# One written order for the transfers of both queues, and the convolution in forty groups of eight tokens

## The chip, the core and the metric

The kernel runs on one core of one Trainium2 chip. Its time is the device time of one execution in microseconds (us). Engines are named as in the profile: PE (matmuls), DVE (vector), ACT (scalar), POOL, and SP, which only issues transfers here. Transfers are issued from two queues, that of SP and that of ACT.

## What is computed

One step of a hybrid decoder layer for 320 tokens of 1024 features: 256 tokens of one prompt (T columns 0 to 255) and eight samples of eight tokens (columns 256 to 319). The layer is attention over blocks of cached keys and values beside a state-space mixer (SSD), then cross attention to a memory, then a squared-ReLU MLP. The x, B and C rows of the mixer go through a causal depthwise convolution of width 4 before the scan; each sequence starts from its own history of three rows (zeros for the prompt, a cached state for each sample), and the last three raw rows of each sequence are an output:

```python
def causal_conv(xbc, buf, w, bias):
    t = xbc.shape[1]
    full = jnp.concatenate([buf.astype(xbc.dtype), xbc], axis=1)
    y = bias
    for i in range(CONV_W):
        y = y + full[:, i:i + t] * w[i]
    return y, full[:, full.shape[1] - (CONV_W - 1):]
...
x ; x += W_out[concat(MoBA heads, Mamba-2 SSD heads)](rmsnorm(x)) ; x += memory cross-attention(rmsnorm(x), rmsnorm(mem)) ; x += squared-ReLU MLP(rmsnorm(x))
```

## The kernel before

Features lie on the 128 partitions and tokens along the columns. Every gemm multiplies a weight chunk of 128 x 1024 values with eight tiles of 128 x 320. To keep float32 accuracy both sides are split into a rounded part and a remainder, and each product takes three matmuls (`gemm3`, L389 to L391: high by high, high by low, low by high).

A weight chunk of 512 KB is brought by `load` (L331) into one of three buffers `wr`. ACT then makes the rounded part `wh` (L383) and DVE the remainder `wl` (L384). Chunks 5 to 47 are issued from ACT's queue, ahead of the instructions that ACT has behind them, the others from SP's. Cached keys (`ckT`) and values (`cv`) of the sample attention come in 256 KB pieces through SP (L827, tile `kv`).

The program up to the MLP is written as some twenty streams that yield after each portion: V the value projection, Q the query and key gemms, F the query and key factors, S and T the attention of the samples and of the prompt, B the gemms of the x, B and C rows, Z those of the gate, D and R the scan, O and J the output projection, others for memory and cross attention. The string `ORDER` says which stream goes on next (`weave_by`); that sets PE's order. For ACT and DVE two further tables, `ACT_ORDER` and `DVE_ORDER`, give the order of all their instructions. At the end `_issue_order` puts the instructions of one engine in that order. Each engine takes its instructions in that order, and one that waits holds all behind it. ACT's queue of transfers is part of this: a weight issue that has to wait holds the activations behind it.

A transfer signals its landing on one of eight completion semaphores (DMAHW0 to DMAHW7), which are handed out in turn to the transfers of both queues in the order in which the scheduler lists them. A transfer is issued when the one that had the same semaphore before it, eight places ahead in that list, has landed, and when its buffer is free.

For each of its eight tiles of 128 rows, stream B ends in `xbc_done` (L981 on): DVE scales the gemm's result into a row of raw values (L988 for the prompt, L989 for the samples with their eleven columns each), POOL puts the history in and takes the output rows out (L987, L990, L991), ACT starts the sum with the first tap (Identity, L994), DVE adds three taps (L996), ACT makes the tanh (L998), and DVE multiplies (L1003 prompt, L1004 samples).

Other lines that the prediction speaks of: L367 transposes on PE, of the rows s4 that ACT copies (`rows_out`, L505 and L507) or of the sample attention's yn (ACT, L956); L500 sums of squares on PE; L868 the samples' scores on PE, after DVE's block mask m (L872); L893 the samples' probabilities p on ACT; L784 to L790 the prompt's exponentials tq; L881 and L607 small DVE steps of the scores and of the key factors (ts); L1065 PE's first use of the last convolution tiles.

## Time and profile before

| | us |
|---|---|
| median of 3 runs | 520.6 |
| lowest and highest | 519.11, 522.63 |
| profiled execution | 520.65 |
| span of that execution in the trace | 518.9 |
| busy: PE, DVE, ACT, POOL | 501.1, 343.4, 251.5, 48.4 |

The span runs from the first to the last recorded instruction of the program; 1.75 us of the profiled execution lie around it. A row of a group shows its line, engine and operation, what it writes and reads with the shape, how often, then the sum of its time (us) and the mean of one (ns), and behind the last bar the idle time ahead of it and what ended it. A row of the chain shows a start, a length and what ran. The granted clock of PE is full (1.00) throughout.

### The profile page before, as it was taken

Reading aid. Unit: us, or ns where it says so; the run is one execution under the profiler, and the core shown is the slowest. Engines: PE = TensorE matmul, PEld = TensorE weight load, DVE = VectorE, ACT = ScalarE, POOL = GpSimd, SP = SyncE. Lnnn points to the kernel's source line nnn. Section 1 sums busy time; section 2 is a strip of 40 time slices with the busy share of each in tenths; the row PEclk is TensorE's granted clock in tenths of the full one; section 3 lists DMA queues with packets and bytes.
Section 4 is the critical chain, followed back from the end, with each engine's and each line's share of the span. In section 5 each row is a group of like instructions: output and inputs, shape, how many; then the busy total and the mean of one; then the engine's idle time right before and its main releaser. Section 6 shows DMA issues by size and latency. Waiting matters only on the chain.

```text
span 518.9 us, 10547 instructions
## 1 busy us (share of the span) xinstructions
PE 501.1 (97%) x3954; PEld 453.6 (87%) x3954; DVE 343.4 (66%) x713; ACT 251.5 (48%) x512; POOL 48.4 (9%) x98
## 2 busy tenths in 40 slices
PE   8999899997989999999899999999999999999997
PEld 5988677876758799999579899999999999999997
DVE  6867699668668598965748779776766434334431
ACT  7524346947767775735466444343434322332330
POOL 2500000120100000000000122231312000000000
PEclk9999999999999999999999999999999999999999
DMA  8889998999799434796922366564644444544520
GB/s 288 314 304 377 392 351 289 338 329 365 279 377 346 139 123 163 242 332 215 378 93 85 121 248 205 162 222 143 227 140 157 162 147 163 176 149 161 176 95 13
DMA packets 45364, 116.53 MB, mean 225 GB/s; under 512 B 5058, under 2 KB 7234, under 8 KB 45314
## 3 DMA queue, kind: packets, MB, share of 16 engines
q1 hardware_dynamic: 39266, 94.37, 52.8%
q10 hardware_dynamic: 6048, 21.50, 11.5%
q8 instruction: 31, 0.51, 0.4%
q14 instruction: 19, 0.16, 0.1%
HBM read 109.71 MB, written 6.14 MB: 223 GB/s over the span
## 4 chain that ended last, share of the span: by engine, by line
PE 78%; DVE 8%; ACT 6%; DMA 5%; issue 2%; SPq 0%; ACTq 0%; POOL 0%; POOLq 0%
PE mm L389 21%; PE mm L390 20%; PE mm L391 20%; DMA kv<-ckT 3%; PE ms L367 2%; ACT wh L383 2%; DVE wl L384 2%; DMA wr<-w 2%; PE as L921 2%; PE sc L706 1%; PE as L367 1%; PE ms L534 1%; PE sc L868 1%; PE mm L1623 1%; PE sc L1549 1%
## 5 line engine op out<-in xcount | busy, mean ns | idle before, releaser
L383 ACT ACTIVATE wh<-wr 128x1024 fp32r<-128x1024 f32 (+1 forms) x115 | 118.8, 1036 | 175.0 <-PE mm L390 104.9
L384 DVE TENSOR_TENSOR wl<-wr,wh 128x1024 fp32r<-128x1024 f32 (+1 forms) x115 | 144.7, 1261 | 83.5 <-ACT wh L383 81.0
L389 PE MATMUL mm<-big,wh 128*128 128x320 f32 x544 | 171.9, 316 | 2.4 <-DVE t L881 0.7
L390 PE MATMUL mm<-big,wh 128*128 128x320 f32 x544 | 168.2, 309 | 0.0
L391 PE MATMUL mm<-big,wl 128*128 128x320 f32 x544 | 168.2, 309 | 0.0
L389 PEld LDWEIGHTS mm<-big,wh 128*128 128x128 f32 x544 | 102.2, 188 | 9.6 <-issue 5.7
L390 PEld LDWEIGHTS mm<-big,wh 128*128 128x128 f32 x544 | 102.2, 188 | 0.8 <-DVE big L1611 0.3
L391 PEld LDWEIGHTS mm<-big,wl 128*128 128x128 f32 x544 | 102.1, 188 | 0.2 <-DVE wl L384 0.2
L391 PE MATMUL mm<-hh,wl 128*128 128x320 f32 x256 | 78.9, 308 | 0.0
L390 PE MATMUL mm<-hl,wh 128*128 128x320 f32 x256 | 78.9, 308 | 0.0
L389 PE MATMUL mm<-hh,wh 128*128 128x320 f32 x256 | 78.9, 308 | 0.0
L390 PEld LDWEIGHTS mm<-hl,wh 128*128 128x128 f32 x256 | 48.1, 188 | 0.0
L389 PEld LDWEIGHTS mm<-hh,wh 128*128 128x128 f32 x256 | 48.1, 188 | 0.0
L391 PEld LDWEIGHTS mm<-hh,wl 128*128 128x128 f32 x256 | 48.1, 188 | 0.0
L1686 POOL TENSOR_TENSOR t<-t 128x320 f32<-128x320 f32 x32 | 27.8, 869 | 171.3 <-DVE t L1683 162.4
L1683 DVE SCALAR_TENSOR_TENSOR t<-mm,rb 128x320 f32<-128x320 f32 x32 | 15.7, 489 | 15.3 <-PE mm L391 14.8
L996 DVE SCALAR_TENSOR_TENSOR t<-t,cwh,t 128x344 f32<-128x344 f32 x24 | 13.8, 573 | 7.7 <-ACT t L994 7.3
L868 PE MATMUL sc<-kv,qs 128*32 128x256 f32 x256 | 15.9, 381 | 2.3 <-DVE m L872 2.3
L1687 DVE TENSOR_TENSOR hl<-t,hh 128x320 fp32r<-128x320 f32 x32 | 15.4, 481 | 2.5 <-POOL t L1686 2.5
L1684 ACT ACTIVATE hh<-t 128x320 fp32r<-128x320 f32 x32 | 14.6, 458 | 2.5 <-DVE t L1683 2.5
L921 PE MATMUL as<-kv,p 128*32 128x256 f32 x256 | 15.9, 382 | 0.0
L1349 DVE TENSOR_TENSOR x2T<-mm,x2T 128x320 f32<-128x320 f32 x8 | 3.9, 492 | 17.8 <-PE mm L391 17.8
(358 smaller groups left out, 624.0 us busy)
## 6 DMA issues: line engine op xcount, KB each, us to landing
wr<-w SPq DMA_DIRECT2D x69, 512.0 KB, 3.5
wr<-w ACTq DMA_DIRECT2D x41, 512.0 KB, 5.6
kv<-ckT SPq DMA_DIRECT2D x64, 256.0 KB, 5.3
kv<-cv SPq DMA_DIRECT2D x64, 256.0 KB, 5.8
kv<-mk SPq DMA_DIRECT2D x8, 512.0 KB, 6.1
kv<-mv SPq DMA_DIRECT2D x8, 512.0 KB, 7.8
kv<-h SPq DMA_DIRECT2D x4, 512.0 KB, 7.7
big<-h SPq DMA_DIRECT2D x4, 512.0 KB, 5.3
```

Source lines behind the costliest of these rows:

```text
L367: PE.transpose(out, in_, ident[:n, :n])
L383: A.activation(hi[:, c], raw[:, c], AF.Copy)
L384: V.tensor_tensor(lo[:, c], raw[:, c], hi[:, c], op=ALU.subtract)
L389: PE.matmul(out, hi[:, cols], xh, start=start, stop=False)
L390: PE.matmul(out, hi[:, cols], xl, start=False, stop=False)
L391: PE.matmul(out, lo[:, cols], xh, start=False, stop=stop)
L868: PE.matmul(ps[r:r + 32, 256 * n:256 * n + 256], qs[:, s, g, b0 + e, :], kbs[e][:, :, 128 * (2 * g + s):128 * (2 * g + s) + 128], start=s ...
L921: PE.matmul(yv[r:r + 32, 0:256], pT[:, 2 * n + q, r:r + 32], vbs[e][:, q, 256 * g:256 * g + 256], start=n == 0 and q == 0, stop=first and ...
L1683: V.scalar_tensor_tensor(t, ps[:, :T], 0.0, rb3, op0=ALU.max, op1=ALU.mult)
L1684: A.activation(hh[:, m, :], t, AF.Square)
L1686: G.tensor_tensor(f, t, t, op=ALU.mult)
L1687: V.tensor_tensor(hl[:, m, :], f, hh[:, m, :], op=ALU.subtract)
```

## The change

There are three parts.

The new table `DMA_ORDER` lists the transfers of both queues in one order, and `_issue_order` is called for them as well; it takes a condition in place of an engine. So the table decides which earlier transfer each one takes its semaphore from.

`xbc_done` lays the raw values out as 40 groups of 11 columns, each with three columns of history and eight tokens; the 256 prompt tokens are 32 such groups. The history of the prompt's groups 1 to 31 is the end of the group before and is copied by ACT (a new instruction of 128 x 31 x 3). One DVE product fills all groups. The sum starts with the last tap in place of the first, and all steps run over 320 columns where they ran over 344; the last product is one instruction where it was two. POOL has three copies and fills a tile where it had four.

`ORDER`, `ACT_ORDER` and `DVE_ORDER` are new. Lines below the tables stand four further down (L331 is L335 after the change, L383 is L387, L505 is L509, L956 is L960).

```diff
@@ -67,45 +67,49 @@
...
-ORDER = ("VVFVVQQQQQQQQQQQQQQQVFVQFVQFFQQQQFVQQQQQSSQQQFSSQQZQZQSSFSFSSSFFBBBBSZBBSBBFSBBTZSBSSBBBSSTBBTBTBBSS"
...
-ACT_ORDER = ("1 0 2 19 3+1 20 6 5 7 21 8+3 22 12+3 23 16+2 24+2 28 30 33 32 27 37 34 29 43 38 31 50 39 44 36 35 53 59 40+1 "
...
+ORDER = ("FVVVVQQQQQQQQQQQQQVQQFVQFVFQFQQQFVQQQQQSSQQQFSSQQQZQZSSFSFSVSSQFFBBBBSZBSBFBBSBBTZSBSSBBBSSBBTBTTBBS"
...
+ACT_ORDER = ("1 0 2 19 3+1 20 6 5 7 21 8+1 22 10+5 23 18 16+1 24+2 28 30 33 32 27 37 34 29 47 38 31 50 41 48 36 35 57 39+1 "
...
+DMA_ORDER = ("0+15 19+1 16+2 21+2 29+1 27 31+6 28 38+16 64 24 55+1 65 25 66 57+4 75 26 62 67+6 84 74 76+7 63 86+1 85 88+3 "
...
@@ -235,9 +239,9 @@
     return out
 
 
-def _issue_order(tc, nc, eng, runs):
-
-    ins = [i for i in nc.cur_bb.bb.instructions if i.engine == eng and i.is_tile_traced]
+def _issue_order(tc, nc, take, runs):
+
+    ins = [i for i in nc.cur_bb.bb.instructions if i.is_tile_traced and take(i)]
     ins = [ins[i] for i in _runs(runs)]
     info = mybir.DependencyInfo(mybir.DependencyClass.NoSync, mybir.DependencyReason.DATA)
     for a, b in zip(ins, ins[1:]):
@@ -981,27 +985,20 @@
     def xbc_done(m):
         def done(ps):
             cvo = made["cvo"]
-            raw = tm(347)
-            rs3 = raw[:, 259:347].rearrange("p (b t) -> p b t", t=11)
-            G.memset(raw[:, 0:3], 0.0)
-            G.tensor_copy(rs3[:, :, 0:3], scv[:, 24 * m:24 * m + 24].rearrange("p (b t) -> p b t", t=3))
-            V.tensor_tensor(raw[:, 3:259], ps[:, :TP], rb[:, :TP], op=ALU.mult)
-            V.tensor_tensor(rs3[:, :, 3:11], by_seq(ps[:, TP:T]), by_seq(rb[:, TP:]), op=ALU.mult)
-            G.tensor_copy(cvo[:, m, 0:3], raw[:, 256:259])
-            G.tensor_copy(cvo[:, m, 3:27].rearrange("p (b t) -> p b t", t=3), rs3[:, :, 8:11])
-
-            y = tm(344)
-            A.activation(y, raw[:, 0:344], AF.Identity, scale=cwh[:, 4 * m:4 * m + 1], bias=cwh[:, 32 + m:33 + m])
-            for w in range(1, 4):
-                V.scalar_tensor_tensor(y, raw[:, w:w + 344], cwh[:, 4 * m + w:4 * m + w + 1], y, op0=ALU.mult, op1=ALU.add)
-            th = tm(344)
+            raw = tm(440).rearrange("p (g t) -> p g t", t=11)
+            G.memset(raw[:, 0, 0:3], 0.0)
+            G.tensor_copy(raw[:, 32:40, 0:3], scv[:, 24 * m:24 * m + 24].rearrange("p (b t) -> p b t", t=3))
+            V.tensor_tensor(raw[:, :, 3:11], by_seq(ps[:, :T]), by_seq(rb), op=ALU.mult)
+            G.tensor_copy(cvo[:, m, :].rearrange("p (b t) -> p b t", t=3), raw[:, 31:40, 8:11])
+
+            y = tm(T)
+            A.activation(raw[:, 1:32, 0:3], raw[:, 0:31, 8:11], AF.Copy)
+            A.activation(by_seq(y), raw[:, :, 3:11], AF.Identity, scale=cwh[:, 4 * m + 3:4 * m + 4], bias=cwh[:, 32 + m:33 + m])
+            for w in range(3):
+                V.scalar_tensor_tensor(by_seq(y), raw[:, :, w:w + 8], cwh[:, 4 * m + w:4 * m + w + 1], by_seq(y), op0=ALU.mult, op1=ALU.add)
+            th = tm(T)
             A.activation(th, y, AF.Tanh)
-
-            def smp(t):
-
-                return t[:, 256:344].rearrange("p (b t) -> p b t", t=11)[:, :, 3:11]
-            V.scalar_tensor_tensor(cv[:, m, :TP], th[:, :TP], 1.0, y[:, :TP], op0=ALU.add, op1=ALU.mult)
-            V.scalar_tensor_tensor(by_seq(cv[:, m, TP:]), smp(th), 1.0, smp(y), op0=ALU.add, op1=ALU.mult)
+            V.scalar_tensor_tensor(cv[:, m, :], th, 1.0, y, op0=ALU.add, op1=ALU.mult)
             if m == 7:
                 S.dma_start(O["conv"], cvo)
         return done
@@ -1730,9 +1727,10 @@
                 gemm3(ps[:, :T], w, slice(k * P, k * P + P), hh[:, kt, :], hl[:, kt, :], kt == 0, kt == 31)
         residual(m, None, None, None)(ps)
         S.dma_start(O["yT"][:, m, :], xT[:, m, :])
-    for eng, runs in ((mybir.EngineType.Activation, ACT_ORDER), (mybir.EngineType.DVE, DVE_ORDER)):
+    for take, runs in ((lambda i: i.engine == mybir.EngineType.Activation, ACT_ORDER), (lambda i: i.engine == mybir.EngineType.DVE, DVE_ORDER),
+                       (lambda i: i.opcode == "DMACopy", DMA_ORDER)):
         if runs:
-            _issue_order(tc, nc, eng, runs)
+            _issue_order(tc, nc, take, runs)
     stD.close()
     ctx.close()
 
```

The tables move rows. First ACT at the early query and key gemms, about 27 to 41 us into the profiled execution; wr are weight transfers, wh conversions, s4 the copies for PE's first factor transposes, and the brackets name what a row waits for. Before:

```order
L383 ACTIVATE wh_79_435<-wr_78_433 128x1024 [waits DMAHW6_49,PE_49]
L474 ACTIVATE sq_62_344<-mm_58_313 128x320 [waits PE_49]
L331 DMA wr_102_581<-w 128x1024 [waits DVE_49]
L383 ACTIVATE wh_83_450<-wr_82_448 128x1024 [waits DMAHW7_49,PE_49]
L383 ACTIVATE wh_94_516<-wr_93_514 128x1024 [waits DMAHW0_49,PE_49]
L635 ACTIVATE rb_31_179<-ms_77_428 128x320 [waits PE_49]
L474 ACTIVATE sq_74_420<-mm_63_348 128x320
L331 DMA wr_115_684<-w 128x1024 [waits DMAHW7_49,DVE_49]
L331 DMA wr_131_768<-w 128x1024 [waits DMAHW2_49,DVE_49]
L505 ACTIVATE s4_86_465<-ms_85_460 128x320 [waits PE_49]
L507 ACTIVATE s4_86_465<-ms_85_460 128x64
```

After the change:

```order
L387 ACTIVATE wh_79_435<-wr_78_433 128x1024 [waits DMAHW6_49,PE_49]
L478 ACTIVATE sq_62_344<-mm_58_313 128x320 [waits PE_49]
L335 DMA wr_102_581<-w 128x1024 [waits DMAHW2_49,DVE_49]
L387 ACTIVATE wh_85_458<-wr_84_456 128x1024 [waits DMAHW7_49,PE_49]
L387 ACTIVATE wh_96_544<-wr_95_542 128x1024 [waits PE_49]
L639 ACTIVATE rb_31_179<-ms_77_428 128x320 [waits PE_49]
L478 ACTIVATE sq_74_420<-mm_63_348 128x320
L335 DMA wr_127_743<-w 128x1024 [waits DMAHW2_49,DVE_49]
L509 ACTIVATE s4_82_452<-ms_81_447 128x320 [waits PE_49]
L511 ACTIVATE s4_82_452<-ms_81_447 128x64
L335 DMA wr_131_768<-w 128x1024 [waits DMAHW3_49,DVE_49]
```

Three weight issues in a row, wr_95 (a row above these, on DMAHW2 too), wr_102 and wr_127, now use one semaphore, where wr_93, wr_102 and wr_115 had three; and one issue, not two, stands between sq and s4.

Next ACT at the sample and prompt attention, 90 to 117 us. Before the change, wr_296 was issued among the prompt's exponentials:

```order
L784 ACTIVATE tq_203_1134,psm_201_1130<-tq_203_1134,pmx_200_1129,fqs_28_176 128x128
L383 ACTIVATE wh_256_1477<-wr_255_1475 128x1024 [waits PE_49]
L331 DMA wr_296_1735<-w 128x1024 [waits DMAHW5_49,DVE_49]
L790 ACTIVATE tq_202_1131<-tq_202_1131,psm_201_1130 128x256 [waits DVE_49]
L784 ACTIVATE tq_205_1142,psm_201_1130<-tq_205_1142,pmx_200_1129,fqs_28_176 128x128 [waits DVE_49]
L785 ACTIVATE tq_205_1142,psm_201_1130<-tq_205_1142,pmx_200_1129,fqs_28_176 128x256
```

Its conversion and the next weights came some thirty rows later, among the Identity (L994) and tanh (L998) of the convolution's tiles; the last issue, wr_465, stands ahead of an Identity:

```order
L331 DMA wr_342_2009<-w 128x1024 [waits DMAHW6_49,DVE_49]
L998 ACTIVATE t_241_1398<-t_240_1393 128x344 [waits DVE_49]
L331 DMA wr_403_2313<-w 128x1024 [waits DMAHW1_49,DVE_49]
L994 ACTIVATE t_251_1462<-t_250_1455,cwh_22_158 128x344 [waits DVE_49,Activation_49,Pool_49]
L956 ACTIVATE yn_267_1560<-as_258_1487,rs_236_1361 128x256 [waits PE_49]
L383 ACTIVATE wh_319_1870<-wr_318_1868 128x1024 [waits DMAHW0_49,PE_49]
L998 ACTIVATE t_252_1467<-t_251_1462 128x344 [waits DVE_49]
L808 ACTIVATE big_5_84<-ms_271_1584 128x2x256 [waits PE_49]
L967 ACTIVATE big_5_84<-as_272_1594 64x2x16 [waits PE_49]
L967 ACTIVATE big_5_84<-as_272_1594 64x2x16 x3
L331 DMA wr_465_2584<-w 128x1024 [waits DMAHW2_49,DVE_49]
L994 ACTIVATE t_269_1575<-t_268_1568,cwh_22_158 128x344 [waits DVE_49,Activation_49,Pool_49]
```

After the change the issues and the conversion stand close together, and Identity (L996) and history copy (L995) are ahead of the issue of wr_468:

```order
L387 ACTIVATE wh_293_1712<-wr_292_1710 128x1024 [waits DMAHW4_49]
L335 DMA wr_296_1723<-w 128x1024 [waits DMAHW1_49]
L335 DMA wr_316_1844<-w 128x1024 [waits DMAHW2_49]
L1000 ACTIVATE t_239_1381<-t_238_1375 128x320 [waits DVE_49]
L335 DMA wr_346_2021<-w 128x1024 [waits DMAHW7_49,DVE_49]
L995 ACTIVATE t_250_1447<-t_250_1447 128x31x3 [waits DVE_49]
L996 ACTIVATE t_251_1452<-t_250_1447,cwh_22_158 128x320 [waits DVE_49]
```

The rows of ACT right behind these, after the change:

```order
L387 ACTIVATE wh_297_1725<-wr_296_1723 128x1024 [waits DMAHW1_49]
L1000 ACTIVATE t_252_1458<-t_251_1452 128x320 [waits DVE_49]
L960 ACTIVATE yn_267_1550<-as_258_1477,rs_236_1355 128x256 [waits PE_49]
L387 ACTIVATE wh_317_1846<-wr_316_1844 128x1024 [waits DMAHW2_49,PE_49]
L995 ACTIVATE t_268_1558<-t_268_1558 128x31x3 [waits DVE_49,Activation_49]
L996 ACTIVATE t_269_1563<-t_268_1558,cwh_22_158 128x320 [waits Activation_49]
L335 DMA wr_403_2297<-w 128x1024 [waits DMAHW5_49]
L812 ACTIVATE big_5_84<-ms_271_1572 128x2x256 [waits PE_49]
L971 ACTIVATE big_5_84<-as_272_1582 64x2x16 [waits PE_49]
L971 ACTIVATE big_5_84<-as_272_1582 64x2x16 x3
L335 DMA wr_468_2586<-w 128x1024 [waits DMAHW7_49,DVE_49]
```

The issue of wr_296 moved from some thirty rows to six rows ahead of its conversion, and yn follows that conversion; no issue stands directly ahead of an Identity here.

Last ACT at the end of the convolution, 135 to 144 us. Before:

```order
L331 DMA wr_495_2710<-w 128x1024 [waits DMAHW2_49,DVE_49]
L994 ACTIVATE t_323_1917<-t_322_1910,cwh_22_158 128x344 [waits DVE_49,Pool_49]
L383 ACTIVATE wh_466_2586<-wr_465_2584 128x1024 [waits PE_49]
L1185 ACTIVATE sq_419_2397<-big_5_84 128x8x8 [waits DVE_49]
L1043 ACTIVATE bt_340_2006<-ms_339_2003 128x256 [waits PE_49]
L331 DMA wr_499_2736<-w 128x1024 [waits DMAHW1_49,DVE_49]
L998 ACTIVATE t_324_1922<-t_323_1917 128x344 [waits DVE_49]
L1015 ACTIVATE t_336_1986<-t_335_1984 128x320 [waits DVE_49]
```

After the change:

```order
L1000 ACTIVATE t_314_1840<-t_313_1834 128x320 [waits DVE_49]
L995 ACTIVATE t_322_1896<-t_322_1896 128x31x3 [waits DVE_49]
L996 ACTIVATE t_323_1901<-t_322_1896,cwh_22_158 128x320
L1182 ACTIVATE sq_422_2395<-big_5_84 128x8x8 [waits DVE_49]
L335 DMA wr_484_2673<-w 128x1024 [waits DMAHW2_49,DVE_49,Activation_49]
L387 ACTIVATE wh_469_2588<-wr_468_2586 128x1024 [waits DMAHW7_49,PE_49]
L1000 ACTIVATE t_324_1907<-t_323_1901 128x320 [waits DVE_49,Pool_49]
L1040 ACTIVATE bt_344_2018<-ms_343_2015 128x256 [waits PE_49]
L1012 ACTIVATE t_340_1998<-t_339_1996 128x320 [waits DVE_49,Activation_49]
L335 DMA wr_491_2697<-w 128x1024 [waits DMAHW7_49,DVE_49]
```

The tanh of the last tile (t_324) has the issue of wr_499, on DMAHW1, right ahead before; after the change that issue's successor wr_491 stands behind it, and wr_484, on DMAHW2, two rows ahead.

More of the change, by code (lines that the diff above doesn't have):

```diff
@@ L69 @@
 PACE = 1.3
[L70 to L74 removed]
[14 rows of a table removed]
[L89 removed]
[19 rows of a table removed]
+ORDER = ("FVVVVQQQQQQQQQQQQQVQQFVQFVFQFQQQFVQQQQQSSQQQFSSQQQZQZSSFSFSVSSQFFBBBBSZBSBFBBSBBTZSBSSBBBSSBBTBTTBBS"
+         "SBSBSSBBSSSBTSSTBZSZBBSSBBTBTSZBBTSTBDSSSSZSDZSZDDZDSSZSDSDDSDTDDZZDDSDSZDDSZRSSSSSRSSRRMORORWRORWRO"
+         "OWNOOWNONOOOOOMOONNOWONJJJJJJJJZJJJJJMWJJKOJKKKKKKKKKKGKKKKKWGMXGacJMGGGGGGGMGWGGGGGGMXXbcXXaabcadcb"
+         "cbabbaacMbcaddcddadcdGGKGGGGWGGGGGGGGGGG")
+ACT_ORDER = ("1 0 2 19 3+1 20 6 5 7 21 8+1 22 10+5 23 18 16+1 24+2 28 30 33 32 27 37 34 29 47 38 31 50 41 48 36 35 57 39+1 "
[14 rows of a table added]
+DVE_ORDER = ("0+2 17 4 3 5 18 6+1 19 8 10+1 9 12+1 20 14+1 21 16 22+2 27 32 35 25+1 36 28 30 29 31 53 33+1 37 39 38 40+8 54 "
[18 rows of a table added]
+DMA_ORDER = ("0+15 19+1 16+2 21+2 29+1 27 31+6 28 38+16 64 24 55+1 65 25 66 57+4 75 26 62 67+6 84 74 76+7 63 86+1 85 88+3 "
[4 rows of a table added]
 TAKEN = []
```

4 lines of the change are left out of this document (removed), and 69 rows, old and new, of tables (ACT_ORDER, DMA_ORDER, DVE_ORDER).

## Prediction

> **What bounds the kernel now.** I begin with the page's head: how busy each engine is, and over which stretch the transfers are dense.
>
> ```profile
> PE 501.1 (97%) x3954; PEld 453.6 (87%) x3954; DVE 343.4 (66%) x713; ACT 251.5 (48%) x512; POOL 48.4 (9%) x98
> DMA  8889998999799434796922366564644444544520
> GB/s 288 314 304 377 392 351 289 338 329 365 279 377 346 139 123 163 242 332 215 378 93 85 121 248 205 162 222 143 227 140 157 162 147 163 176 149 161 176 95 13
> ```
>
> PE is busy for 501.1 of 518.9 us, so all waits of PE together are 17.8 us; nothing that only relieves DVE or ACT can be worth more than the PE waits that those two end. The DMA digits are 8 or 9 for the first thirteen slices (some 170 us) and low after that. Next the stretches, with PE's busy time in each:
>
> ```profile
> 20.00:60.00 40.00, 37.85 (x287) 32.63 (x286) 28.66 (x70) 13.67 (x21) 0.26 (x2) 1.00 0.97 347
> 60.00:100.00 40.00, 37.32 (x380) 29.44 (x379) 34.51 (x118) 25.71 (x78) 2.35 (x15) 1.00 0.95 339
> 100.00:130.00 30.00, 27.04 (x300) 20.46 (x299) 21.18 (x59) 18.93 (x53) 5.54 (x19) 1.00 0.96 337
> 130.00:170.00 40.00, 38.08 (x390) 28.51 (x393) 30.53 (x69) 28.50 (x79) 2.53 (x9) 1.00 0.90 328
> 170.00:240.00 70.00, 70.00 (x542) 64.12 (x532) 55.43 (x127) 41.42 (x86) 0.15 (x1) 1.00 0.58 204
> 240.00:290.00 50.00, 46.73 (x441) 40.08 (x440) 33.98 (x91) 30.38 (x74) 0.00 (x0) 1.00 0.52 185
> 290.00:510.00 220.00, 220.00 (x1517) 218.90 (x1517) 124.21 (x154) 77.19 (x94) 27.80 (x32) 1.00 0.50 165
> ```
>
> The second column is PE. From 170 to 240 and from 290 to 510 it never stops, and the clock is 1.00: no order of other engines can shorten those 290 us. PE idles 2.15 + 2.68 + 2.96 + 1.92 = 9.7 us between 20 and 170, and 3.3 us from 240 to 290. Those **13.0 us** are all that the change can win; the rest of the 17.8 is the start and the last output. The list of PE's waits says what ends them:
>
> ```profile
> PE sc L868 <- DVE m L872: 2.3, 2, 1.8
> PE ms L1065 <- DVE big L1003: 1.7, 1, 1.7
> PE as L367 <- ACT p L893: 1.3, 3, 0.5
> PE ms L367 <- DVE ts L607: 0.9, 1, 0.9
> PE mm L389 <- DVE t L881: 0.7, 1, 0.7
> ```
>
> The two largest sit behind one pattern. The chain that ended last, at 107 to 117 us and at 138 to 144 us, with the DVE row of the timeline between:
>
> ```profile
> 107.47 8.39 DMA kv<-ckT
> 115.93 0.33 ACTq L331
> 116.39 0.68 ACT t L994
> 117.09 0.58 DVE L996 SCALAR_TENSOR_TENSOR t<-t,cwh,t 128x344 f32<-128x344 f32 x1 [3.87 <-ACT t L994]
> 138.42 4.55 DMA kv<-ckT
> 143.44 0.50 ACT t L998
> 143.96 0.44 DVE big L1003
> 144.44 0.49 PE ms L1065 x2
> ```
>
> In the first (**stall A**) a cached-key transfer issued by SP at 107.47 lands at 115.9. ACT's weight issue (L331) uses the completion semaphore of that transfer, so it can't be issued before; ACT takes its instructions in order, so the Identity of the convolution (L994) waits behind the issue, DVE waits 3.87 us for it, and PE waits 1.8 us for the scores' mask work m that DVE does next, then 0.7 for t, and some 0.4 for p. In the second (**stall B**) the tanh (L998) stands behind such an issue, and PE waits 1.7 us for the last convolution tile. ACT is only half busy; it isn't slow, it is parked.
>
> **The change, part by part.**
>
> *The two parked issues.* In the changed order the Identity and history copy of the tile at stall A stand ahead of the next weight issues (wr_403 and wr_468), and wr_468 takes the turn of a weight that was issued some 10 us before, not of a fresh key load. Stall A: 1.8 + 0.7 + 0.4 = **−2.9 us**. DVE got its operand 3.87 us late and PE lost 1.8, so about 2.1 us of slack are left before another lateness shows. At stall B the last tile's tanh stands ahead of the weight issue that would hold it (wr_491): **−1.7 us**. Neither can give more than this, nor less than nothing by itself. Late next at stall A are the exponentials of tq, which ACT makes right after and which end the 0.4 for p.
>
> *The early weights.* The price of the new turns: wr_95, wr_102 and wr_127, three consecutive issues of ACT, now share one completion semaphore, so each waits until the one before has landed. wr_127 stands right ahead of the copy s4 (L505, after the change L509) for which PE's L367 waits.
>
> ```profile
> 23.54 8.08 DMA wr<-w
> 36.13 0.75 PE L500 MATMUL ms<-sq,cst 128*32 128x320 f32 x8
> 37.60 0.55 PE L367 MATMUL ms<-cst,s 128*128 128x128 f32 x3 [0.72 <-ACT s L505]
> DMA to landing us min/median/max: 3.4/5.6/8.9
> ```
>
> The last row is for all weights from ACT's queue. wr_95 is third in ACT's line, as the transfer of the first row was, and lands at 31.6. wr_102 then lands at 35.0, 37.2 or 40.5 by the smallest, median and largest time. wr_127 is issued (0.33 us), s4 is copied (0.45), and L367 can start at 35.8, 38.0 or 41.3. PE has its inputs otherwise at 36.9 (36.13 + 0.75). Before it waited 0.72, so the difference is −0.7, +0.4 or +3.7. I take **+0.4**, the median row. SP gains here what ACT loses: its key loads no longer take the turn of a weight, which hides nothing that PE waited for, and I give it nothing.
>
> *The clustered late weights.* wr_296, wr_316 and wr_346 are issued together just behind the conversion of wr_293, and wr_296 is converted six rows later, with yn (L956) right behind, for which PE's L367 waits.
>
> ```profile
> 102.86 2.00 ACT L383 ACTIVATE wh<-wr 128x1024 fp32r<-128x1024 f32 x2
> 105.36 0.33 ACTq L331 DMA_DIRECT2D wr<-w  x1
> 111.54 0.44 PE L367 MATMUL as<-cst,yn 128*128 128x128 f32 x2
> ```
>
> Before, both conversions (wr_293 and wr_296) ran at 102.86; now wr_296 is only issued when the first is done, at 103.9 (half of 2.00 later), and lands at 107.3, 109.5 or 112.8. Conversion 1.06, tanh about 0.47 and yn 0.48 add 2.0: PE could go on at 109.3, 111.5 or 114.8, against 111.54 before: 0, 0 or +3.3. The key loads that now go ahead of it make the middle row optimistic; I take **+0.8**, and keep both ends. Queued behind the waiting conversion on ACT are the tanh of the next tile, yn, and wr_316's conversion; PE waits for the second of these, and through it the gemms do.
>
> *The k factors.* The copy of the key sums now stands behind a p transpose copy and a weight conversion that it preceded. Nothing to one conversion (1.06 us) is its price on the wait for ts (L607, 0.9 us in the list of waits); the middle, **+0.5**.
>
> *The convolution itself*, from groups by form:
>
> ```profile
> L988 DVE TENSOR_TENSOR t<-mm,rb 128x256 f32<-128x256 f32 x8 | 3.4, 421 | 0.2
> L989 DVE TENSOR_TENSOR t<-mm,rb 128x64 f32<-128x64 f32 x8 | 1.7, 213 | 0.0
> L996 DVE SCALAR_TENSOR_TENSOR t<-t,cwh,t 128x344 f32<-128x344 f32 x24 | 13.8, 573 | 7.7 <-ACT t L994 7.3
> L1003 DVE SCALAR_TENSOR_TENSOR big<-t,t 128x256 f32<-128x256 f32 x8 | 3.3, 417 | 2.4 <-ACT t L998 2.4
> L1004 DVE SCALAR_TENSOR_TENSOR big<-t,t 128x64 f32<-128x64 f32 x8 | 1.8, 220 | 0.0
> L527 DVE SCALAR_TENSOR_TENSOR big<-x2T,prm,big 128x320 fp32r<-128x320 f32 x8 | 4.3, 543 | 1.0 <-ACT big L526 1.0
> L994 ACT ACTIVATE t<-t,cwh 128x344 f32<-128x344 f32 x8 | 5.4, 670 | 6.2 <-DMA kv<-ckT 3.7 <-POOL cvo L990 1.7 <-DVE t L989 0.8
> L998 ACT ACTIVATE t<-t 128x344 f32<-128x344 f32 x8 | 3.9, 487 | 7.8 <-DMA kv<-ckT 3.4 <-DVE tq L776 3.1 <-DVE t L996 1.2
> L1449 ACT ACTIVATE tq<-mm,prm 128x64 f32<-128x64 f32 x4 | 1.3, 315 | 1.1 <-DVE qz L1445 1.1
> ```
>
> DVE a tile before: 421 + 213 + 3·573 + 417 + 220 = 2990 ns. After: one product of 320 elements, 421 + 64·(421−213)/192 = 490; three accumulations at the 543 ns of L527's form; a last one of 417 + 64·(417−220)/192 = 483: 2602 ns. Over 8 tiles that is **−3.1 us of DVE**. ACT before: 670 + 487 = 1157. After: 24 elements less on each take some 24 ns off, 646 + 463, and the history copy of 93 elements is new: no such row exists; the nearest is L1449 (64 elements, 315 ns), and I take 320 between nothing and 670: 1429, over 8 tiles **+2.2 us of ACT**. One tile's path is shorter by 388 − 272 = about 0.1 us. Beyond stall B no row shows PE waiting for the convolution, and DVE is 60 to 85% busy beside a PE that has gemms to do, so all this counts **0**; with that cover gone, the 3.1 would be the most it gives, and 2.2 the most it costs.
>
> L1004 walks eight groups of 8 words with a hop of 11 and takes 220 ns for 64 elements, where the slope from L1003 to a contiguous row would be about the same: no price of the hop shows. The Trainium skill ("Vector Engine (DVE) Microarchitecture Reference", 5.2 Measured stream behaviour on trn2) speaks against the grouped form: full rate needs runs of adjacent words that start on an 8-byte boundary, and pairs that start on an odd word took 1.30 ns a column for 1.054. Groups of 11 words start on an odd word every second time; an estimate by that page puts some 79 ns on each accumulation at the worst, 1.9 us of DVE's gain, and three of them (0.24 us) on the path of a tile; the sum would be 517.9 for 517.7. No row of the profile shows three such streams at 320 elements.
>
> **Sum.** The profiled execution took 520.65 us (span 518.9 and 1.75 around it), 0.05 from the median of the runs, 520.6. 520.65 − 2.9 − 1.7 + 0.4 + 0.8 + 0.5 = 517.75; less the 0.05, **517.7 us**. With the unknown prices at their ends the forecast's own range runs from 520.6 − 4.6 − 0.7 = 515.3 to 520.6 − 4.6 + 3.7 + 1.1 = 520.8 (not with both landings late at once, which is the third rival).
>
> **Rivals.**
>
> 1. *The new orders close more than the two stalls.* 13.0 − 4.6 = 8.4 us of PE idle stay in the movable stretches; the waits for p, ts, and the exchange of rows in the cross attention (240 to 290 us, 3.3 us idle) are all waits for an instruction that stood in the wrong place. If half of them go: 520.6 − 4.6 − 4.2 = **511.8**. For it: almost every row of the orders is new, and key loads run ahead freely. Against: some of the new places I could follow are worse, not better.
>
> 2. *The transfers set the pace and the waits only move.* From 20 to 130 us the DMA engines are 95 to 97% busy at 337 to 347 GB/s. Were that all they can do, a wait taken from ACT's issue would return as a wait for the bytes: **520.6**. Against it: the fifth slice reached 392 GB/s, and stall A's PE waits were for an engine parked behind an issue, not for bytes. The Trainium skill ("DMA: Bandwidth & Descriptors", Specifications) gives about 358 GB/s as a core's limit at its memory; by that the stage would hold at most 5 us, and this rival would be the likeliest. The trace's 392 lies above the limit, so the trace decides.
>
> 3. *Weights that wait for weights* (slower). Key loads no longer wait for weights, so they go first, and chained weights land late, near 8.9 us: +3.7 at 37 us, +3.3 at 111 us, +1.06 for the k factors, and ACT held up at 111 us hands half of stalls A and B back (4.6 / 2 = 2.3 kept): 520.6 + 8.1 − 2.3 = **526.4**. It decides at a landing later than 5.6 us at the second place, and later than 5.2 at the first (36.9 + 0.72 − 0.33 − 0.45 − 31.6). The median lies on that edge, and one in the chain took 8.08.
>
> **Chances.** Forecast 0.46; rival 1 0.22; rival 2 0.16; rival 3 0.16. A difference under 1% (5.2 us) is about what a measurement of this kernel can't tell from none. Faster by more (under 515.4): most of rival 1 and the lower edge of the forecast, 0.25. Slower by more (over 525.8): two thirds of rival 3, and orders worse than I followed, 0.13. Within: 0.62. The range takes in rival 1 without its lower tail and stops short of rival 3's end: 511.5 to 525.
>
> **What would show it.** Stalls: no ACT wait for ckT over 2 us at the convolution's Identity or tanh, and PE's waits for m (L872) and the last convolution product under 0.5 us. Early: the idle time ahead of the L367 at 37 us is 0.5 to 2 us, released by the copy s4. Late weights: a wait of ACT for a weight at the conversion around 105 to 112 us, with yn behind it. Convolution: accumulations near 543 ns, not 620; DVE's total about 3 us lower, ACT's some 2 us higher. PE still without idle from 170 to 240 and from 290 on. Wrong I would be if PE's idle sum outside stalls A and B moved by more than 3 us either way, which is a matter of landing times that the trace of before can't show for another order of issue.

## The result, and the profile after

| | before | after |
|---|---|---|
| median, us | 520.63 (6 runs) | 514.41 (6 runs) |
| lowest and highest, us | 519.11, 524.42 | 513.22, 517.27 |
| profiled execution, us | 520.65 | 513.36 |
| its span, us | 518.9 | 511.6 |

The ratio is 0.9877, with a 95% interval from 0.9833 to 0.9921: the change makes the kernel 1.2% faster, 6.2 us. That is 3.3 us more than forecast, inside the stated range, below the forecast's own range (515.3 to 520.8), and on the side that had a chance of 0.25.

The head of the page of the changed kernel, and its stretches (stretch, PE, PEld, DVE, ACT and POOL busy, granted clock, DMA share, GB/s):

```profile
PE 499.2 (98%) x3954; PEld 452.5 (88%) x3954; DVE 342.1 (67%) x697; ACT 252.4 (49%) x520; POOL 47.8 (9%) x90
```

```profile
20.00:60.00 40.00, 38.17 (x290) 32.56 (x290) 30.20 (x78) 14.21 (x24) 0.26 (x2) 1.00 0.99 358
60.00:100.00 40.00, 38.56 (x397) 31.59 (x396) 33.72 (x108) 27.57 (x84) 2.94 (x15) 1.00 0.96 337
100.00:130.00 30.00, 29.12 (x317) 21.95 (x317) 20.79 (x50) 22.10 (x64) 4.45 (x11) 1.00 0.98 362
130.00:170.00 40.00, 38.90 (x436) 27.84 (x432) 32.09 (x71) 27.10 (x79) 1.80 (x8) 1.00 0.93 338
170.00:240.00 70.00, 70.00 (x490) 65.71 (x489) 55.20 (x121) 41.90 (x79) 0.15 (x1) 1.00 0.59 200
240.00:290.00 50.00, 48.16 (x460) 42.55 (x459) 36.56 (x101) 29.80 (x75) 1.55 (x2) 1.00 0.49 173
```

PE's idle time (span less busy) is 12.4 us for 17.8: 5.4 of the 7.3 us by which the span is shorter. The other 1.9 is PE's busy sum, 499.2 for 501.1, with the same 3954 matmuls. It isn't the new PE order that does this: a kernel with PE's order of before, told of last among the experiments, has 499.2 too. In the stretches the idle time fell from 2.15 to 1.83 (20 to 60 us), from 2.68 to 1.44, from 2.96 to 0.88, from 1.92 to 1.10, and from 3.27 to 1.84 (240 to 290). Work has moved over the borders of the stretches meanwhile, so these differences say where to look, not what was saved there.

What ends PE's waits now (the list of waits: total, how many, the longest):

```profile
PE ms L371 <- ACT s L509: 1.8, 2, 1.2
PE ms L371 <- DVE ts L611: 1.4, 2, 0.8
...
PE mm L393 <- DVE t L991: 0.8, 1, 0.8
...
PE sc L872 <- DVE m L876: 0.4, 1, 0.4
```

The wait for the mask m went from 2.3 to 0.4, and the waits for the last convolution tile (big, 1.7) and for p (1.3) are out of the list. Beside a wait of 1.4 for POOL in the first 20 us, which both kernels have, the longest is now the one for the early copy s4, 1.2 for 0.7, as the prediction expected. Four places of the timeline answer the steps of the prediction: the early copy, the conversion at 53 us with what PE does after it, and the late weights (start, length, engine, line, operation; in brackets the idle time ahead and what ended it):

```profile
37.41 0.33 ACTq L335 DMA_DIRECT2D wr<-w  x1
37.79 0.44 ACT L509 ACTIVATE s<-ms 128x320 f32<-128x320 f32 x1 [3.05 <-DMA wr<-w]
38.28 0.55 PE L371 MATMUL ms<-cst,s 128*128 128x128 f32 x3 [1.23 <-ACT s L509]
...
53.30 1.06 ACT L387 ACTIVATE wh<-wr 128x1024 fp32r<-128x1024 f32 x1 [3.36 <-PE mm L394]
...
62.63 0.75 PE L673 MATMUL ms<-sq,cst 128*32 128x320 f32 x8
...
99.83 0.34 ACTq L335 DMA_DIRECT2D wr<-w  x1
...
101.09 1.11 ACT L387 ACTIVATE wh<-wr 128x1024 fp32r<-128x1024 f32 x1
...
105.23 1.04 ACT L387 ACTIVATE wh<-wr 128x1024 fp32r<-128x1024 f32 x1
...
107.57 0.46 ACT L960 ACTIVATE yn<-as,rs 128x256 f32<-128x256 f32 x1
...
109.23 0.44 PE L371 MATMUL as<-cst,yn 128*128 128x128 f32 x2
```

The two rows in the middle, 53.30 and 62.63, have counterparts in the kernel before that the prediction had not looked at. The first row here is a weight issue, that of wr_192, just ahead of the conversion:

```profile
55.28 0.33 ACTq L331 DMA_DIRECT2D wr<-w  x1
55.72 1.06 ACT L383 ACTIVATE wh<-wr 128x1024 fp32r<-128x1024 f32 x1 [3.75 <-PE sc L868]
...
64.55 0.74 PE L669 MATMUL ms<-sq,cst 128*32 128x320 f32 x8
```

L669 before is L673 after: PE reaches the same sums of squares at 62.63 for 64.55 and has won 1.9 us already, while the early copy has cost it. The conversion is 2.4 us earlier. In the row of before the profile names PE's scores as what ended ACT's 3.75 us. The issue in front of it tells another tale, which the experiments take up. What this place cost PE is spread over small waits, here those of before from 44 to 66 us:

```profile
PE as L367 <- ACT p L893: 0.9, 2, 0.5
PE sc L868 <- DVE m L872: 0.6, 1, 0.6
PE mm L389 <- DVE kT L585: 0.5, 1, 0.5
```

Four waits, none above 0.6, sum to 2.0 us. In the changed kernel none of them is left.

The steps of the convolution, by form:

```profile
L998 DVE SCALAR_TENSOR_TENSOR t<-t,cwh,t 128x320 f32<-128x320 f32 x24 | 13.2, 549 | 4.4 <-ACT t L996 2.3 <-ACT t L995 1.7
L996 ACT ACTIVATE t<-t,cwh 128x320 f32<-128x320 f32 x8 | 5.3, 664 | 0.1
L1001 DVE SCALAR_TENSOR_TENSOR big<-t,t 128x320 f32<-128x320 f32 x8 | 3.9, 488 | 0.6 <-ACT t L1000 0.5
L991 DVE TENSOR_TENSOR t<-mm,rb 128x320 f32<-128x320 f32 x8 | 3.9, 485 | 0.1
L1000 ACT ACTIVATE t<-t 128x320 f32<-128x320 f32 x8 | 3.8, 470 | 5.2 <-DVE t L998 5.2
L995 ACT ACTIVATE t<-t 128x93 f32<-128x93 f32 x8 | 2.4, 305 | 1.7 <-DVE t L991 1.7
```

A tile takes DVE 485 + 3·549 + 488 = 2620 ns for 2990, and ACT 664 + 470 + 305 = 1439 for 1157.

### The profile page after: what moved, and what is told of

Read it like the earlier page. It is cut to its first block, busy times and chain, and to the rows that moved or that the text cites. A ratio compares the mean times of both kernels' runs of the same rounds, so it can differ in the third digit from the quotient of the medians.

```text
span 511.6 us, 10525 instructions
## 1 busy us (share of the span) xinstructions
PE 499.2 (98%) x3954; PEld 452.5 (88%) x3954; DVE 342.1 (67%) x697; ACT 252.4 (49%) x520; POOL 47.8 (9%) x90
## 4 chain that ended last, share of the span: by engine, by line
PE 84%; ACT 6%; DVE 5%; DMA 2%; issue 1%; SPq 0%; ACTq 0%; DVEq 0%
PE mm L393 22%; PE mm L394 21%; PE mm L395 21%; PE as L925 2%; PE sc L872 2%; DMA wr<-w 2%; PE ms L371 2%; PE as L371 1%; ACT wh L387 1%; DVE wl L388 1%; PE sc L710 1%; PE sc L1546 1%; PE sc L1548 1%; PE as L1570 1%; PE mm L1620 1%
## 5 line engine op out<-in xcount | busy, mean ns | idle before, releaser
L387 ACT ACTIVATE wh<-wr 128x1024 fp32r<-128x1024 f32 (+1 forms) x115 | 118.9, 1037 | 173.6 <-PE mm L394 103.8
L998 DVE SCALAR_TENSOR_TENSOR t<-t,cwh,t 128x320 f32<-128x320 f32 x24 | 13.2, 549 | 4.4 <-ACT t L996 2.3
L1346 DVE TENSOR_TENSOR x2T<-mm,x2T 128x320 f32<-128x320 f32 x8 | 3.9, 492 | 17.8 <-PE mm L395 17.8
```

Of the source, the lines that this page charges most:

```text
L387: A.activation(hi[:, c], raw[:, c], AF.Copy)
```

## The experiments

Each kernel was timed beside the kernel before on the same chip; its medians in the four sessions were 520.88, 520.06, 520.12 and 521.03 us. Kernels that start from before and get a list of transfers have their lines two further down than before. Tables are shown by the rows that they move, since their numbers tell nothing.

### Parts of the change: the list, the convolution, the two issues

**The change without its list of transfers.** The semaphores then go round in the scheduler's own order:

```diff
-    for take, runs in ((lambda i: i.engine == mybir.EngineType.Activation, ACT_ORDER), (lambda i: i.engine == mybir.EngineType.DVE, DVE_ORDER),
-                       (lambda i: i.opcode == "DMACopy", DMA_ORDER)):
+    for take, runs in ((lambda i: i.engine == mybir.EngineType.Activation, ACT_ORDER), (lambda i: i.engine == mybir.EngineType.DVE, DVE_ORDER)):
```

> The changed kernel without the list of transfers: new row orders and new convolution, but the scheduler hands out the completion semaphores itself. Theory 1 (the new places of rows do the work; the list only keeps some issues from being parked): 515 to 517, with one or two weight issues of ACT waiting for a fresh key load again between 100 and 140 us, and PE's wait for s4 at 38 us shorter than 1.4. Theory 2 (the list of transfers is the gain): 519 to 521, stalls A and B of the kernel before are back.

515.4 us, ratio 0.989 [0.985, 0.993]; the changed kernel has 0.9877 [0.9833, 0.9921]. The list's own share can't be told from nothing. In the profile two effects stand against each other. PE's early transposes start at 37.10 in place of 38.28, because wr_127 no longer waits for a weight. Later ACT is parked twice behind issues that wait for cached keys and values:

```profile
110.61 0.60 ACT L812 ACTIVATE big<-ms 128x512 f32<-128x512 f32 x1 [1.80 <-DMA kv<-ckT]
...
113.15 0.47 ACT L1000 ACTIVATE t<-t 128x320 f32<-128x320 f32 x1 [1.50 <-DMA kv<-cv]
```

So most of the gain is in the orders of the engines' rows, and the list trades an early wait for later ones.

**The kernel before with only the two issues freed.** A list that is before's own order, but for two transfers that stand a few places further ahead, so that they take another semaphore. No row of any engine moves; the transfers that the two pass shift by one place:

```diff
+DMA_ORDER: before's own order; wr_465 at place 125 for 130, wr_499 at 157 for 161
-L331 DMA wr_465_2584<-w 128x1024 [waits DMAHW2_49,DVE_49]
+L333 DMA wr_465_2584<-w 128x1024 [waits DMAHW5_49,DVE_49]
-L331 DMA wr_499_2736<-w 128x1024 [waits DMAHW1_49,DVE_49]
+L333 DMA wr_499_2736<-w 128x1024 [waits DMAHW5_49,DVE_49]
```

> The kernel before with its own order of transfers written out, in which only the two weight issues of stalls A and B (wr_465, wr_499) are moved 5 and 4 places ahead, so that they take the semaphores of transfers that landed long before. Theory 1: both parked issues go, 516 to 517 (4.6 us at most), no wait of the Identity or tanh for a key load over 1 us, PE's waits for m and for the last convolution product under 0.5 us. Rival (the waits only move, since the transfers set the pace): 520 to 521, with other waits of PE in the same stretch.

516.44 us, 0.9903 [0.9865, 0.9941]: −4.4 us by the medians, where the prediction's two stalls sum to −4.6. The wait for m at stall A is gone from the list and so is the one for the last convolution tile; a part comes back at the step right behind, where PE waits for bt. The wait for t, which the prediction had counted to stall A, stays at its 0.7. The two stretches (columns as above) have less idle time than before, by 2.2 and 0.8 us:

```profile
PE ms L1082 <- ACT bt L1045: 0.9, 1, 0.9
PE mm L391 <- DVE t L883: 0.7, 1, 0.7
```

```profile
100.00:130.00 30.00, 29.26 (x320) 22.72 (x319) 21.80 (x61) 21.77 (x60) 5.32 (x17) 1.00 0.97 345
130.00:170.00 40.00, 38.89 (x438) 27.55 (x436) 31.56 (x70) 26.56 (x73) 2.52 (x9) 1.00 0.98 353
```

This settles what stalls A and B are: two positions in a list, and no row of any engine, are worth 4.4 us. It speaks against the rival by which the transfers set the pace, since not a byte is moved less. It also leaves some 2 us of the change unexplained. Its timeline holds the clue, for the list shifted what the profile could see:

```profile
55.37 1.06 ACT L385 ACTIVATE wh<-wr 128x1024 fp32r<-128x1024 f32 x1 [3.29 <-DMA out_v<-v]
...
64.19 0.75 PE L671 MATMUL ms<-sq,cst 128*32 128x320 f32 x8
```

This is the conversion that before has at 55.72, and here the profile names a transfer of the output v as what ended ACT's wait.

**The kernel before with the new convolution**, its rows put where those of the old one stood:

```diff
-            raw = tm(347)
...
+            raw = tm(440).rearrange("p (g t) -> p g t", t=11)
...
(xbc_done as in the change; ORDER as before; ACT_ORDER and DVE_ORDER renumbered)
```

> The kernel before with the new convolution alone; the order tables of before are kept, with the history copy right ahead of the Identity and each merged product in the place of one of its two parts. Theory 1 (the convolution is hidden): 520 to 521.5, DVE about 3 us less busy, ACT about 2 us more. Rival (the shorter DVE work pays): 517 to 518.

520.97 us, 1.0011 [0.9985, 1.0037]: nothing. **The changed kernel with the old convolution**, put back in the same way:

```diff
-            raw = tm(440).rearrange("p (g t) -> p g t", t=11)
...
+            raw = tm(347)
...
(xbc_done as before; ORDER and DMA_ORDER as in the change; ACT_ORDER and DVE_ORDER renumbered)
```

> The changed kernel with the old convolution: all three orders of the change, with the old convolution's instructions in the places of the new ones (no history copy, seven DVE instructions a tile). Theory 1: 514 to 515.5, as the changed kernel. Rival (the convolution pays some 3 us): 517 to 518.

513.29 us, 0.9848 [0.981, 0.9885], which is not to be told from the changed kernel. Both ways round the convolution is hidden, as forecast.

### The stretch from 44 to 64 us: two theories that fell, and one that held

What makes the conversion at 55.72 late? First theory: DVE's order, since PE's scores end late there and PE's scores wait for DVE's mask. **The kernel before with the scores' reductions ahead of the key rotations on DVE**:

```diff
 L591 SCALAR_TENSOR_TENSOR t_577<-mm_513,prm_81,rot_102 128x320
+L871 TENSOR_REDUCE gs_636<-sc_635 128x2
+L872 TENSOR_REDUCE m_105_599<-sc_635 128x2
 L589 TENSOR_TENSOR kT_173<-kT_173,t_574 128x320
 L592 TENSOR_TENSOR kT_173<-kT_173,t_577 128x320
 L384 TENSOR_TENSOR wl_771<-wr_768,wh_770 128x1024
-L871 TENSOR_REDUCE gs_636<-sc_635 128x2
-L872 TENSOR_REDUCE m_105_599<-sc_635 128x2
```

> The kernel before with two DVE rows moved: the first two reductions of the samples' scores (gs and m, L871 and L872) go ahead of two key rotations (L589, L592) and a weight remainder (L384), as they stand after the change. Theory (this place is where the unforecast 2.5 us between 53 and 64 us come from): 518 to 519.5, PE's waits for m at 54 us and for p at 62 to 64 us gone, PE 1.5 to 2.5 us earlier at 65 us. Rival (the gain there comes from key loads that land earlier, since SP no longer waits for weights): 520 to 521, and PE at 65 us as before.

522.09 us, 1.0032 [1.0002, 1.0063]: no gain, rather a small loss. The scores no longer wait at that place, but a new wait takes over, and the conversion comes at 56.49, later than before:

```profile
PE mm L389 <- DVE kT L585: 1.7, 1, 1.7
```

**The same rows together with the two freed issues**:

```diff
+DMA_ORDER: as with the two issues freed
 (DVE's rows as in the kernel above)
```

> The kernel before with the two moved weight issues and the two moved DVE rows together, so old convolution, old PE and ACT orders. Theory (three places carry most of the change): 4.1 + 2, so 514 to 515, as the changed kernel. Rival (they don't add up, the second stall only shows what the first hid): 516 to 517.

516.38 us, 0.9923 [0.9898, 0.9948]; the two issues alone had 0.9903. The DVE rows add nothing. Even with them the conversion, at 54.47, is ended by the transfer of v.

Second theory: the issue of wr_170, some rows ahead, parks the copies of the values, so the output v starts late. **The kernel before with that issue moved behind the value copies and a conversion**:

```diff
-L331 DMA wr_170_956<-w 128x1024
 L713 ACTIVATE v_174<-sc_188,rt_178 128x512 x2
 L715 ACTIVATE ts_547<-as_189 64x512
 L383 ACTIVATE wh_686<-wr_684 128x1024
+L331 DMA wr_170_956<-w 128x1024
```

> The kernel before with one ACT row moved: the issue of wr_170 (issued at 46.0 us, when a key load's semaphore came free) stands behind the value copies L713, L715 and one conversion, as after the change, not ahead of L713. Theory (a third parked issue is where the 2.5 us between 53 and 64 us come from): ACT copies v at 44 us instead of 46.4, DVE no longer idles 2 us for ts, PE is 1.5 to 2.5 us earlier at 65 us, time 518 to 519. Rival (that gain needs the new PE order or the key loads that run ahead): 520 to 521, PE at 65 us within 0.5 of before.

521.06 us, 1.0006 [0.9976, 1.0036]: nothing. The first copies of the values start earlier, at 44.57 for 46.41, but the issue now goes out at 49.64 and holds the last of them, which comes at 50.02 for 49.14. The conversion is not earlier but later, with a cached-value transfer named:

```profile
57.33 1.06 ACT L383 ACTIVATE wh<-wr 128x1024 fp32r<-128x1024 f32 x1 [4.26 <-DMA kv<-cv]
```

**That move together with the two freed issues**:

```diff
+DMA_ORDER: as with the two issues freed
 (ACT's rows as in the kernel above)
```

> The kernel before with all three weight issues moved (wr_170 behind the value copies, wr_465 and wr_499 ahead in the list of transfers), old convolution and old orders otherwise. Theory (the three parked issues carry nearly the whole change): 4.1 + 2, so 514 to 515. Rival (the first gain is given back in the transfer-bound stretch, as with s4 in the changed kernel): 516 to 517.

516.26 us, 0.9919 [0.9892, 0.9947]: nothing beyond the two issues either. Whatever the rows ahead did, ACT was idle for 3.3 to 5.2 us ahead of the conversion, and in all four of these kernels and in the one with only the two issues freed the profile names a landing. That leaves the issue right in front of it, wr_192. It uses DMAHW0, and ACT takes no conversion before it is out. **The kernel before with wr_192 alone at another place of the list**:

```diff
+DMA_ORDER: before's own order; wr_192 at place 59 for 64
-L331 DMA wr_192_1090<-w 128x1024 [waits DMAHW0_49,DVE_49]
+L333 DMA wr_192_1090<-w 128x1024 [waits DMAHW3_49,DVE_49]
```

> The kernel before with its own order of transfers written out and one weight issue (wr_192) five places ahead: it no longer takes the semaphore of a piece of the output v (issued at 48.9, landed at 55.2), behind which ACT's conversion at 55.7 stood. Theory (this parked issue alone makes the waits for the key rotation at 59 us and for p at 62 to 64 us): conversion at 53.7 to 54.5, PE 1 to 2 us earlier at 65 us, 518.5 to 519.5. Rival (it takes the rows of the whole stretch): PE at 65 us within 0.5 of before, 520 to 521.

518.69 us, 0.9961 [0.9933, 0.9988]: faster by 2.0 us by the ratio (2.3 by the medians), with one transfer put five places ahead. The timeline shows the mechanism:

```profile
52.66 0.34 ACTq L333 DMA_DIRECT2D wr<-w  x1
...
53.09 1.06 ACT L385 ACTIVATE wh<-wr 128x1024 fp32r<-128x1024 f32 x1 [1.85 <-DVE wl L386]
...
61.92 0.75 PE L671 MATMUL ms<-sq,cst 128*32 128x320 f32 x8
```

The issue goes out at 52.66 for 55.28, the conversion follows at 53.09 for 55.72, and PE is there at 61.92 for 64.55: 2.6 us each time. Of PE's four small waits from 44 to 66 us one is left, of 0.2 for p. So the profile's releaser in the row of before, PE's scores, was not the cause; ACT was parked behind an issue, a third time. In the profiled execution itself the 2.6 us are lost again. Stalls A and B are still in this kernel, and longer than before; behind stall B PE is 1.5 us ahead (142.97 for 144.44), and at 148.3 us it is level, because its granted clock falls in between, which the last section takes up:

```profile
PE sc L870 <- DVE m L874: 2.5, 1, 2.5
PE ms L1067 <- DVE big L1005: 2.2, 1, 2.2
```

Last, **the kernel before with the two issues freed and ACT, DVE and the list in the stretch from 44 to 64 us as the change has them**, but PE's order and the convolution of before:

```diff
+DMA_ORDER: as with the two issues freed; wr_182 at place 56 for 58, wr_192 at 58 for 64
-L331 DMA wr_170_956<-w 128x1024 [waits DMAHW4_49,DVE_49]
 (value copies and the conversion wh_686)
+L333 DMA wr_170_956<-w 128x1024 [waits DMAHW4_49,DVE_49]
+L385 ACTIVATE wh_770<-wr_768 128x1024 [waits DMAHW2_49,PE_49]
 (sq_572; then the issues of wr_182 and wr_192)
-L383 ACTIVATE wh_770<-wr_768 128x1024
 (on DVE: the remainder wl_133 ahead of the key rotations, the scores' first reductions between these)
```

> The kernel before with the two moved issues of stalls A and B, and from 44 to 64 us all that the change has there: ACT's rows (wr_170 behind the value copies, a conversion ahead of the issue of wr_182), DVE's rows (a weight remainder ahead of the key rotations, the scores' first reductions between them), and wr_182 and wr_192 earlier in the list of transfers. Old PE order, old convolution, old orders elsewhere. Theory (the stretch is the other part of the gain, and its rows work only together): PE 2 to 3 us earlier at 65 us than in the kernel before, 513.5 to 515. Rival (the new PE order is needed): PE within 1 us of before at 65 us, 516 to 517.

513.94 us, 0.9885 [0.985, 0.9919]: the time of the change. First two rows of its timeline, then its stretch from 240 to 290 us:

```profile
51.67 1.06 ACT L385 ACTIVATE wh<-wr 128x1024 fp32r<-128x1024 f32 x1 [2.70 <-DMA wr<-w]
...
61.33 0.75 PE L671 MATMUL ms<-sq,cst 128*32 128x320 f32 x8
```

```profile
240.00:290.00 50.00, 46.73 (x445) 40.32 (x444) 34.43 (x98) 29.03 (x72) 1.55 (x2) 1.00 0.49 173
```

The two freed issues and this one stretch give as much as the whole change, without the new `ORDER` and without the new convolution. The share of the stretch is not pinned: the medians of this kernel and of the one with only the two issues freed differ by 2.5 us, their ratios by 0.0018, some 0.9 us, with intervals that overlap. It is not in every place the same way: from 240 to 290 us this kernel idles 3.27 us as before does, where the change idles 1.84; what the change pays for that elsewhere, beyond the early copy's 0.7, was not taken apart.

### The price of the early weights

**The changed kernel with the copies s4 ahead of the issue of wr_127**:

```diff
-L335 DMA wr_127_743<-w 128x1024 [waits DMAHW2_49,DVE_49]
 L509 ACTIVATE s4_82_452<-ms_81_447 128x320 [waits PE_49]
 L511 ACTIVATE s4_82_452<-ms_81_447 128x64
+L335 DMA wr_127_743<-w 128x1024 [waits DMAHW2_49,DVE_49]
```

> The changed kernel with one ACT row moved: the issue of wr_127 stands behind the two copies of s4, not ahead of them. Theory (the chained weight issue parks ACT ahead of s4): PE's wait of 1.2 us for s4 at 38 us is gone and the time is 513 to 513.5, 1.2 less than the changed kernel's. Rival (the weight that is issued later is then late itself): 514 to 515, with a wait for wr_127's conversion between 42 and 50 us.

513.89 us, 0.9871 [0.9827, 0.9914]: not to be told from the changed kernel, though the early wait of 1.2 is gone as intended. PE's transposes start 1.0 us earlier, and about as much is waited at 217 us for the memory keys:

```profile
37.27 0.49 PE L371 MATMUL ms<-cst,s 128*128 128x128 f32 x3
...
217.33 0.39 PE L393 MATMUL mm<-kv,wh 128*128 128x256 f32 x1 [0.96 <-DVE kv L1430]
```

**Two more places changed in the same spirit**, a copy s ahead of a conversion and a product of the convolution ahead of the scores' second reductions:

```diff
 (ACT's rows as in the kernel above)
-L387 ACTIVATE wh_2823<-wr_2821 128x1024
 L509 ACTIVATE s_496_2728<-ms_2723 128x320
 L511 ACTIVATE s_496_2728<-ms_2723 128x64
+L387 ACTIVATE wh_2823<-wr_2821 128x1024
...
+L991 TENSOR_TENSOR t_1829<-mm_1709,rb_179 128x40x8
 L875 TENSOR_REDUCE gs_1637<-sc_1636 128x2
 L876 TENSOR_REDUCE m_273_1589<-sc_1636 128x2
 L883 TENSOR_REDUCE t_306_1800<-gs_1637 128x1
-L991 TENSOR_TENSOR t_1829<-mm_1709,rb_179 128x40x8
```

> The changed kernel with three places mended: wr_127's issue behind the copies of s4; the copies of s4 at 244 us ahead of a weight conversion in place of behind it; and the DVE product of a convolution tile (L991, for whose bank PE waits 0.8 us at 122 us) ahead of the reduction of the scores. Theory (each PE wait that a row's place makes is worth its length): 1.2 + 0.8 + 0.8, so 511.5 to 512.5. Rival (PE waits that go in the transfer-bound stretch come back later): 513 to 514.5.

515.87 us, 0.9913 [0.9878, 0.9947]: no better, rather worse. Of the three waits only the early one is gone. The copy that was moved is another than the one meant: it runs at 184.21 us, ahead of a conversion at 184.64, where the changed kernel has them the other way round and PE does not wait. The copy that PE waits for still stands behind its conversion (246.41 behind 245.44), and the wait is 0.56 as before. The wait for the product at 121 us shrank from 0.82 to 0.65 only, and since the scores' reductions now run behind the product, PE waits 1.4 us for p right after. The wait for the memory keys grew too:

```profile
PE mm L393 <- DVE kv L1430: 2.3, 1, 2.3
PE as L371 <- ACT p L897: 1.4, 1, 1.4
```

So this kernel does not test the place at 244 us. Why the memory keys come later when the early rows are faster was not taken apart; here the conversion that went behind the copy at 184 us is a possible cause beside it. None of the kernels clearly beats the change: 513.29, 513.89 and 513.94 lie within its own interval.

## Why the prediction was right or wrong, by its steps

**Right in kind, too large in size: the two parked issues.** What bounds the kernel was read rightly, and the kernel that frees these two issues and moves no row is 4.4 us faster by the medians, for the −2.9 and −1.7 that were read from PE's waits. But the waits themselves gave only some 3.0 of the 4.6: the idle time of the two stretches fell by 2.2 and 0.8, and in the changed kernel by 2.1 and 0.8. The 0.7 for t was no part of stall A, since that wait is still there when the issue is freed, and of stall B about half, 0.9, comes back at bt; the prediction had let nothing come back there. Of the 4.1 us between the profiled executions of the two kernels, 1.3 are PE's busy sum (499.8 for 501.1), for which no run shows a cause, and over many executions the granted clock adds to the 4.4, as the last section shows. That the measured −4.4 lies so near the −4.6 is in part luck.

**Wrong: the count of the stalls.** The step that failed is the reading of "the two largest sit behind one pattern". The pattern had a third instance at 55 us. The prediction started from the head of PE's list of waits, where this place is spread over four waits that sum to 2.0, and the row at 55.72, which names PE as the releaser, does not show it either. An issue of 0.33 us that ends just before a parked row is the same picture as at 115.93 and 116.39. The runs price it at −2.0 (alone, by the ratio) to −2.6 (by its rows). With 2.5, which is by the medians what the last kernel gains on the one with the two issues freed (516.44 − 513.94), the sum is 517.7 − 2.5 = 515.2, for 514.41 measured. That this is near is not all merit: the stalls gave 1.6 less than priced, the late weights and the k factors cost nothing for the 0.8 + 0.5 charged, and PE's busy sum, which the prediction had taken as fixed, fell by 1.9. Rival 1 had foreseen more closing than the two stalls, at 511.8, but by half of all remaining idle; it was above all one place.

**The early weights: right in kind, short in size.** Forecast +0.4 with L367 at 38.0; measured 38.28, hence +0.68. The list without this chain has PE there at 37.10. Its price in the total is not shown: taking it away changed the time by less than the runs can tell.

**The late weights: +0.8 charged, nothing paid.** The prediction let wr_296 be issued when the conversion ahead of it was done. The issue is at 99.83 and that conversion starts at 101.09: the issue went out 1.26 us before the start, and 2.4 before the end, of a row ahead of it. The conversion follows at 105.23, yn at 107.57, and PE takes yn at 109.23, earlier than the 111.54 of before and after a wait of 0.2 at most.

**The k factors: +0.5 charged, about nothing paid.** The wait for ts of the key factors is 0.8 at 68 us, for 0.9 before. A second wait for ts, 0.6 at 42 us, is new; it belongs to the factors of the queries, and it is there without the list as well.

**The convolution: right.** DVE −3.0 us over the eight tiles for −3.1, ACT +2.3 for +2.2, and in the time 0, shown from both sides. The busy totals of the engines moved less (DVE −1.3, ACT +0.9). For DVE that is the convolution's own doing: the kernel before with nothing but the new convolution has −1.2 too. A total counts the time in which two rows overlap once, so a sum over single rows overstates what an engine wins; DVE's rows of before sum to 372.7 us, for a busy 343.4. The accumulations took 549 ns: 6 more than the contiguous row of before. The Trainium skill ("Vector Engine (DVE) Microarchitecture Reference", 5.2 Measured stream behaviour on trn2) has a dearer column for pairs of words that start on an odd one in both sources; the estimate by it was some 79 ns for each accumulation. Here one source walks the groups, and this trace shows no such price; the sum by that rule, 517.9, was no nearer.

**The rivals.** That the transfers set the pace is refuted by the two freed issues, and by the third. Of the slower rival the first half happened, small (0.68 for up to 3.7), and the second did not. What remains open: the 1.4 us that the change gains from 240 to 290 us with what it pays for them, the 1.9 us in PE's busy sum, the exact share of the stretch from 44 to 64 us, and the list's own share, about 1 us by the medians with intervals that overlap.

## What to carry to other kernels

Before trusting a named releaser, look at the row ahead: a transfer's issue of 0.3 us that ended just before a long idle time was over meant three times here that the engine was parked behind the issue, whoever the row named, and every such place should be sought, not only the two that top the list of waits. Not each is worth time: the issue of wr_170 at 46.02 us made the same picture, and moving it behind the value copies gave nothing (1.0006). Where transfers take completion semaphores in turn, the place of a single transfer in the list can be worth microseconds (2.0 for one, about 4 for two here), more than five vector instructions for seven on an engine that PE does not wait for. A local wait that is mended counts only when the time says so: here an early microsecond was given back 180 us later.
